# Combinations of h formed in place, one row behind each of the first two gates and queries, and convolution taps at 0.61 per us

## The chip, the cores and the metric

The kernel runs on one core of a Trainium2 chip. The metric is the device time of one execution in microseconds; the time of a kernel is the median of several executions. The engines named below are TensorE (PE; PEld is its weight load), VectorE (DVE), ScalarE (ACT), GpSimd (POOL) and SyncE (SP), whose only work here is to issue DMAs. DMAs are issued by SyncE, ScalarE and GpSimd and run on sixteen DMA engines.

## What is computed

One layer of a hybrid decoder on 1024 tokens and 16 meta tokens, model width 1024, in float32:

```python
h = rmsnorm(concat([meta, x]), norm_g)                # 1040 x 1024
glu_a, glu_b, z, q, f, i, g_rec, m_conv, m_rec = split(h @ w_in)   # nine sections of 1024
c = causal_dwconv31(glu_a * sigmoid(glu_b)) + conv_b
y_conv = (silu(layernorm(c)) * silu(z)) @ w_conv_out
f = lb + (1 - lb) * sigmoid(f);  k = 1 - f            # HGRN2, 8 heads of 128
o = recurrence(silu(q), k, decay f, values i)         # per head
y_rec = (group_rmsnorm(o) * silu(g_rec)) @ w_rec_out
x = x + (sigmoid(m_conv) * y_conv + sigmoid(m_rec) * y_rec) @ w_out
return rmsnorm(x, final_g)                            # the 1024 real tokens
```

## The kernel before

Channels lie on the partitions and tokens in the columns. h is kept as eight rows (k = 0 to 7), each 128 partitions x 1056 columns: two halves of 528 columns, the second of which repeats 16 tokens. Every matmul operand is split into a high and a low fp32r part, `hh[k]` and `hl[k]` for h; a product takes three matmuls (high x high, high x low, low x high). Weights come as 512 KB tiles: SyncE loads them into `wraw` (two buffers), ScalarE makes the high part and the negated copy of it, and GpSimd adds the raw tile to that by an accumulating DMA (`load_w`, `split_dma`, L139 to L141, L149).

Almost every larger tile is a slot of one pool, `big`: SLOTS = 35 slots of 128 x 1056 float32. A tile gets a slot when the slot's last user is done, and a DMA that still reads the old tile holds it. PSUM has two pools of four banks, `mm` for projections and `hg` for the recurrence. The compiling framework orders the instructions of every engine once, at compile time; each engine then runs its queue in that order. The order need not be the program's, so a row's place in a queue is read from the trace.

**First stage (up to about 480 us).** A list of jobs is run in order: for head j a gate f (`f_job`, wp[4, j]), a query q (`q_job`, wp[3, j]), for some j a quarter of v; then the first two GLU channels. A job's matmuls are cut into small pieces, and after each `tick()` advances the background work by the TensorE time that the piece takes: the recurrence of the previous heads (`hgrn`, a step each 2.0 us; its first step makes QD at L377, then score matmuls at L342), the convolution taps (`conv_taps`, L648) and sums of weights in DRAM (`weight_sums`, L718 and L720). A gate's four column blocks are evacuated by ScalarE (L575) and VectorE (L576, L578), a query's two by L596 and L597.

**Combinations of h.** The second stage multiplies 2 x 2 blocks of weights by 2 x 2 blocks of h with seven products instead of eight. Block row 1 of h is the rows k = 0 to 3, block row 2 the rows 4 to 7; the block columns are the two halves of 528. The products need four combinations, T4 to T7. `h_sums(k)` forms them for one k: it loads rows k and k + 4 of h from DRAM (`h_d`) into `ha` and `hb`, makes four differences and sums of 528 columns on VectorE (L738 to L741), splits each into high and low part (`tsum`, L135 and L136) and stores it to `t_d` in DRAM (L745). Its four calls are jobs: the first two after the first gate, the other two after the first query. At the end of the first stage `h_load` brings T4, T5 and T6 back into twelve slots `t` (L757), and T7 over the second halves of `hh` and `hl` (L762, L763).

**Second stage.** Sixteen gate units (`gate_unit`, one block of 512 columns) and six GLU units (`glu_unit`, two of 264), each of seven products (`strassen`, L879 to L883). Their pieces of weights are 256 KB. The taps of the eight channels are spread over the units by `tick()` at `CONV_RATE` taps per us of TensorE work (0.5 in the first stage); what is left is done at `drain(cbg)`, just before `ln_stats`. A channel's queue is 30 taps of 1024 columns (L648) and a last step that adds it to `csum`.

Of the kernel before, what the change touches and what calls it, by code (L numbers as in the profile page):

```python
# [8 lines left out]
F32 = mybir.dt.float32  # L9
F32R = mybir.dt.float32r  # L10
# [3 lines left out]
ALU = mybir.AluOpType  # L14
PSUM = bass.MemoryType.PSUM

P = 128
# [5 lines left out]
LH = 528  # L23
LX = 2 * LH
# [7 lines left out]
SLOTS = 35  # L32
NSPILL = 6
HG_GAP = 2.0
CONV_RATE = 0.64
SUM_GAP = 2.05
GLU_OVER = 14
EARLY_RATE = 0.5
# [6 lines left out]
def hybrid_kernel(ctx: ExitStack, tc: tile.TileContext, xT, xtok, wv, wp, wro, wco, wout, prm, fg, msk, out):  # L45
    nc = tc.nc
    act, dve, pe = nc.scalar, nc.vector, nc.tensor
# [6 lines left out]
    dram = ctx.enter_context(tc.tile_pool(name="dram", bufs=1, space=bass.MemoryType.DRAM))  # L54
# [8 lines left out]
    def slot(name, n=LX, dt=F32, parts=P):  # L63
        return big.tile([parts, n], dt, name=name, tag="s")
# [4 lines left out]
    def hg_bank():  # L69
# [23 lines left out]
                      in1=lbm.unsqueeze(1).broadcast_to([P, 2, KT]), op=ALU.subtract)  # L93
# [40 lines left out]
    def split(src, hi, lo):  # L134
        act.copy(out=hi, in_=src)  # L135
        dve.tensor_tensor(out=lo, in0=src, in1=hi.bitcast(F32), op=ALU.subtract)  # L136
# [194 lines left out]
    TT = dve.tensor_tensor  # L331
# [210 lines left out]
    hh, hl, hpair = [], [], []  # L542
    h_d = dram.tile([KT, P, LX], F32, name="h_d")
    jobs = []
# [20 lines left out]
    def f_job(j):  # L565
        def run(w):
            Fg = slot("F", L)
            K = slot("K", L)
            for blk in project(w, hh, hl, FB):
                yield  # L570
                if blk is None:
                    continue
                o, n, ps = blk
                fs = Fg[:, o:o + n]
                act.activation(out=fs, in_=ps[:, 0:n], func=AF.Sigmoid)  # L575
                dve.tensor_scalar(out=fs, in0=fs, scalar1=oml[:, j:j + 1], scalar2=lb[:, j:j + 1],  # L576
                                  op0=ALU.mult, op1=ALU.add)
                dve.tensor_scalar(out=K[:, o:o + n], in0=fs, scalar1=-1.0, scalar2=1.0,  # L578
                                  op0=ALU.mult, op1=ALU.add)
            head[j] = (Fg, K)  # L580
        return run

    def q_job(j):
        def run(w):
            while j > 0 and j - 1 not in placed:
                step(bg)
            QD = qx.tile([P, 3, 512], F32, name="QD", tag="qx")
            for blk in project(w, hh, hl, RB):
                yield
                if blk is None:  # L590
                    continue
                o, n, ps = blk
                h0 = o // 2
                qv = QD[:, 0:2, h0:h0 + n // 2].rearrange("p e j -> p j e")
                psv = ps.rearrange("p (j e) -> p j e", e=2)
                act.activation(out=qv, in_=psv, func=AF.Sigmoid)  # L596
                TT(out=qv, in0=psv, in1=qv, op=ALU.mult)  # L597
            bg.append(hgrn(j, *head.pop(j), QD))
        return run

    def v_job(q):
        def run(ws):
            if not hpair:
                hpair.extend(meta_pair(hh[k], hl[k], f"hpair{k}") for k in range(KT))
            yield from v_quarter(q, ws, hh, hl, hpair, False)
        return run
# [117 lines left out]

    t_d = {i: dram.tile([4, P, LX], F32, name=f"t{i}_d") for i in (4, 5, 6, 7)}
    tt = {4: [], 5: [], 6: []}

    def h_sums(k):  # L730
        def run(w):
            ha, hb = slot("ha"), slot("hb")
            nc.sync.dma_start(out=ha, in_=h_d[k])
            nc.sync.dma_start(out=hb, in_=h_d[k + 4])
            t7 = slot("t7", LH)
            b1, b2 = ha[:, 0:LH], ha[:, LH:LX]
            b3, b4 = hb[:, 0:LH], hb[:, LH:LX]
            TT(out=b1, in0=b1, in1=b2, op=ALU.subtract)  # L738
            TT(out=t7, in0=b4, in1=b2, op=ALU.subtract)
            TT(out=b4, in0=b1, in1=b4, op=ALU.add)  # L740
            TT(out=b3, in0=b4, in1=b3, op=ALU.subtract)  # L741
            for i, src in ((6, b4), (5, b1), (4, b3), (7, t7)):
                t = slot("tsum", dt=F32R).rearrange("p (a n) -> p a n", a=2)
                split(src, t[:, 0], t[:, 1])
                nc.gpsimd.dma_start(out=t_d[i][k], in_=t.rearrange("p a n -> p (a n)").bitcast(F32))  # L745
            yield
        return run

    def h_load():

        for i in (6, 5, 7, 4):
            for k in range(4):
                if i == 7:
                    h_last(k)
                    continue
                t = slot(f"t{i}_{k}", dt=F32R)
                nc.gpsimd.dma_start(out=t, in_=t_d[i][k])  # L757
                tt[i].append(t.rearrange("p (a n) -> p a n", a=2))
        yield

    def h_last(k):
        nc.gpsimd.dma_start(out=hh[k][:, LH:LX], in_=t_d[7][k][:, 0:LH])  # L762
        nc.gpsimd.dma_start(out=hl[k][:, LH:LX], in_=t_d[7][k][:, LH:LX])  # L763

    def drained():
        drain(bg)
# [2 lines left out]

    for j in range(NC):  # L770
        jobs.append(([wp[4, j]], f_job(j)))
        if j == 0:
            jobs.append(([], h_sums(0)))
            jobs.append(([], h_sums(1)))
        jobs.append(([wp[3, j]], q_job(j)))
        if j == 0:
            jobs.append(([], h_sums(2)))
            jobs.append(([], h_sums(3)))
        if j in (2, 4):
            q = j // 2 + 1  # L780
            jobs.append(([wv[q, 0], wv[q, 1]], v_job(q)))
    for j in range(2):
        jobs.append(([wp[1, j]], gb_job(j)))
        if j == 1:
            jobs.append(([], lambda w: drained()))
        jobs.append(([wp[0, j]], ga_job(j)))
    jobs.append(([], lambda w: h_load()))

    for i in range(2):
# [23 lines left out]
    first.close()  # L813
    rate[0] = CONV_RATE

# [509 lines left out]
```

## Time and profile before

| | |
|---|---|
| median of three runs | 1232.61 us (1230.66 to 1234.72) |
| the profiled execution, its own time | 1230.3 us |
| its span from the first to the last instruction | 1228.2 us |
| TensorE busy | 1163.5 us, 95% of the span |
| VectorE busy | 877.1 us, 71% |
| ScalarE busy | 588.0 us, 48% |
| GpSimd busy | 287.6 us, 23% |
| mean granted TensorE clock | 0.981 |

Busy time is a share of one execution. Matmuls are pipelined and their ends are modelled, so a busy TensorE can still be a slow one; the granted clock says at what share of full speed it ran.

### The profile page before, as it was taken

What the parts mean: (1) busy time and instruction counts of PE and PEld (TensorE: products, weight loads), DVE (VectorE), ACT (ScalarE), POOL (GpSimd) and SP (SyncE); (2) the same over time, 40 slices, a digit from 0 to 9 for tenths busy, and PEclk for the clock granted to TensorE, in tenths of its full rate; (3) what the DMA queues carried; (4) which work ended last, traced back from release to release, by engine and by line L of the source; (5) the groups of instructions that cost most, each with busy time, mean ns of one, the idle gap of its engine ahead of it and who ended that gap; (6) DMA issues with size and microseconds to landing.
All of it is one profiled execution on the core that took longest, in us unless ns stands there. A gap on an engine that the chain in (4) does not pass through costs nothing.

```text
span 1228.2 us, 21742 instructions
## 1 busy us (share of the span) xinstructions
PE 1163.5 (95%) x8376; PEld 1008.0 (82%) x8376; DVE 877.1 (71%) x1501; ACT 588.0 (48%) x1063; POOL 287.6 (23%) x376
## 2 busy tenths in 40 slices
PE   8994999989999999699999999999999899999997
PEld 7984789979988898478898978988888678888886
DVE  7457766367366589796999997698989747645444
ACT  7563342433533422377767668585855534323211
POOL 5242021322222233212222222322233231000000
PEclk9996999999999999899999999999999999999999
DMA  6479587999699996988998999988899896545321
GB/s 219 155 229 369 174 217 196 228 225 263 161 222 212 200 199 175 358 222 232 253 241 239 224 232 260 215 217 208 228 232 349 285 272 230 181 121 182 118 86 52
DMA packets 119223, 266.54 MB, mean 217 GB/s; under 512 B 12112, under 2 KB 12496, under 8 KB 119120
## 3 DMA queue, kind: packets, MB, share of 16 engines
q0 software_dynamic: 49264, 123.16, 45.1%
q1 hardware_dynamic: 60496, 125.07, 30.4%
q10 hardware_dynamic: 9360, 16.94, 3.8%
q8 instruction: 65, 1.06, 0.3%
q14 instruction: 38, 0.31, 0.1%
HBM read 169.04 MB, written 95.81 MB: 216 GB/s over the span
## 4 chain that ended last, share of the span: by engine, by line
PE 73%; DVE 11%; DMA 10%; issue 3%; ACT 1%; POOL 1%; SPq 0%; DVEq 0%; POOLq 0%; ACTq 0%
PE mm L320 8%; PE mm L323 8%; PE mm L324 8%; PE hg L879 5%; PE hg L882 5%; PE hg L883 5%; PE mm L883 5%; PE mm L879 5%; PE mm L882 4%; DVE c L648 2%; PE mm L204 2%; PE mm L206 2%; PE mm L205 2%; DMA hb<-h_d 2%; DMA wr<-sum_rec 1%
## 5 line engine op out<-in xcount | busy, mean ns | idle before, releaser
L648 DVE SCALAR_TENSOR_TENSOR c<-glu,pt,c 128x1024 f32<-128x1024 f32 (+10 forms) x240 | 306.3, 1279 | 3.6
L141 POOL DMA_DIRECT2D wl<-wr x129 | 110.9, 897 | 329.2 <-ACT wl L140 255.2
L320 PE MATMUL mm<-hh,whi 128*128 128x264 f32 (+2 forms) x512 | 166.2, 326 | 12.0 <-ACT F L575 11.6
L323 PE MATMUL mm<-hl,whi 128*128 128x264 f32 (+2 forms) x512 | 162.4, 318 | 0.5 <-DVE hl L559 0.5
L324 PE MATMUL mm<-hh,wlo 128*128 128x264 f32 (+2 forms) x512 | 161.1, 315 | 0.0
L139 ACT CAST wh<-wr 128x512 fp32r<-128x512 f32 x129 | 78.1, 618 | 108.4 <-PE hg L882 44.5
L320 PEld LDWEIGHTS mm<-hh,whi 128*128 128x128 f32 x512 | 98.4, 193 | 19.0 <-ACT F L575 11.8
L323 PEld LDWEIGHTS mm<-hl,whi 128*128 128x128 f32 x512 | 98.4, 192 | 6.4 <-DVE hl L559 1.2
L324 PEld LDWEIGHTS mm<-hh,wlo 128*128 128x128 f32 x512 | 98.4, 192 | 5.6
L883 PE MATMUL mm<-hh,wl 128*128 128x512 f32 (+1 forms) x224 | 78.1, 349 | 4.7 <-DMA wl<-wr 4.7
L879 PE MATMUL hg<-hh,wh 128*128 128x512 f32 (+1 forms) x224 | 78.8, 352 | 3.6 <-DVE e L909 3.0
L879 PE MATMUL mm<-hh,wh 128*128 128x512 f32 (+1 forms) x224 | 78.4, 350 | 2.3 <-ACT wh L139 1.9
L140 ACT ACTIVATE wl<-wh 128x512 fp32r<-128x512 f32 x129 | 79.6, 629 | 1.7
L883 PE MATMUL hg<-hh,wl 128*128 128x512 f32 (+1 forms) x224 | 78.4, 350 | 0.4 <-DVE wl L136 0.4
L882 PE MATMUL hg<-hl,wh 128*128 128x512 f32 (+1 forms) x224 | 78.5, 350 | 0.0
L882 PE MATMUL mm<-hl,wh 128*128 128x512 f32 (+1 forms) x224 | 78.0, 348 | 0.0
L135 ACT CAST wh<-wr 128x512 fp32r<-128x512 f32 x63 | 38.7, 619 | 51.5 <-PE mm L323 29.2
L879 PE MATMUL hg<-t,wh 128*128 128x512 f32 (+1 forms) x168 | 58.9, 351 | 1.7 <-DMA t<-t_d 1.7
L883 PE MATMUL mm<-t,wl 128*128 128x512 f32 (+1 forms) x168 | 58.9, 351 | 1.0 <-DMA wl<-wr 1.0
L879 PE MATMUL mm<-t,wh 128*128 128x512 f32 (+1 forms) x168 | 59.0, 351 | 0.8 <-ACT wh L135 0.8
L882 PE MATMUL mm<-t,wh 128*128 128x512 f32 (+1 forms) x168 | 58.9, 350 | 0.0
L882 PE MATMUL hg<-t,wh 128*128 128x512 f32 (+1 forms) x168 | 58.7, 349 | 0.0
(346 smaller groups left out, 3095.7 us busy)
## 6 DMA issues: line engine op xcount, KB each, us to landing
wl<-wr POOLq DMA_DIRECT2D x129, 256.0 KB, 5.0
wr<-in_wp_dram SPq DMA_DIRECT2D x66, 256.0 KB, 3.9
wlo<-wraw POOLq DMA_DIRECT2D x24, 512.0 KB, 7.3
wraw<-in_wp_dram SPq DMA_DIRECT2D x20, 512.0 KB, 5.8
t_d<-tsum POOLq DMA_DIRECT2D x16, 528.0 KB, 7.9
sum_rec<-in_wp_dram SPq DMA_DIRECT2D x16, 512.0 KB, 10.5
sum_z<-in_wp_dram SPq DMA_DIRECT2D x16, 512.0 KB, 8.0
wr<-sum_rec SPq DMA_DIRECT2D x32, 256.0 KB, 4.2
```

What stands on the lines that cost most here:

```text
L135: act.copy(out=hi, in_=src)
L139: act.copy(out=hi, in_=src)
L140: act.activation(out=lo, in_=hi.bitcast(F32), func=AF.Copy, scale=-1.0)
L141: nc.gpsimd.dma_start(out=lo, in_=src, accum_op=ALU.add)
L204: pe.matmul(ps, lhsT=a, rhs=whi, start=first, stop=False, **kw)
L320: mm = pe.matmul(ps[:, 0:n], lhsT=a, rhs=xh[k][:, o:o + n], start=(k == 0), stop=False)
L323: pe.matmul(ps[:, 0:n], lhsT=a, rhs=xl[k][:, o:o + n], start=False, stop=False)
L324: last[:] = [pe.matmul(ps[:, 0:n], lhsT=b, rhs=xh[k][:, o:o + n], start=False, stop=(k == KT - 1))]
L648: dve.scalar_tensor_tensor(out=dst, in0=a[:, p0 - d:L - d], scalar=cw[:, j, TAPS - 1 - d:TAPS - d], in1=dst, op0=ALU.mult, op1=ALU.add)
L879: mm = pe.matmul(ps[c], lhsT=a, rhs=xh, start=start and k == 0, stop=False, skip_group_check=True)
L882: pe.matmul(ps[c], lhsT=a, rhs=xl, start=False, stop=False, skip_group_check=True)
L883: pe.matmul(ps[c], lhsT=b, rhs=xh, start=False, stop=k == 3, skip_group_check=True)
```

## The change

`h_sums` no longer takes a seventh slot for T7: all four combinations replace the blocks of `ha` and `hb` that they come from, so `ha` ends as T5 and T7 and `hb` as T4 and T6. Each of the two tiles is then split in one piece of 1056 columns: ScalarE casts it into a slot `tsum`, which is stored as the high part, and VectorE subtracts that from the tile in place, which is stored as the low part. A row takes four slots. `t_d` becomes one tensor in which the two combinations of a tile lie side by side, so a load of T4, T5 or T6 reads two pieces of 528 columns a partition.

The four rows are placed differently among the jobs: one behind the first gate, one behind the first query, one behind the second gate, one behind the second query. `CONV_RATE` goes from 0.64 to 0.61.

```diff
--- before.py
+++ after.py
@@ -32,7 +32,7 @@
 SLOTS = 35
 NSPILL = 6
 HG_GAP = 2.0
-CONV_RATE = 0.64
+CONV_RATE = 0.61
 SUM_GAP = 2.05
 GLU_OVER = 14
 EARLY_RATE = 0.5
@@ -724,7 +724,9 @@
 
 
 
-    t_d = {i: dram.tile([4, P, LX], F32, name=f"t{i}_d") for i in (4, 5, 6, 7)}
+
+    t_d = dram.tile([4, P, 4, 2, LH], F32, name="t_d")
+    place = {5: (0, 0), 7: (0, 1), 4: (2, 0), 6: (2, 1)}
     tt = {4: [], 5: [], 6: []}
 
     def h_sums(k):
@@ -732,35 +734,34 @@
             ha, hb = slot("ha"), slot("hb")
             nc.sync.dma_start(out=ha, in_=h_d[k])
             nc.sync.dma_start(out=hb, in_=h_d[k + 4])
-            t7 = slot("t7", LH)
             b1, b2 = ha[:, 0:LH], ha[:, LH:LX]
             b3, b4 = hb[:, 0:LH], hb[:, LH:LX]
             TT(out=b1, in0=b1, in1=b2, op=ALU.subtract)
-            TT(out=t7, in0=b4, in1=b2, op=ALU.subtract)
+            TT(out=b2, in0=b4, in1=b2, op=ALU.subtract)
             TT(out=b4, in0=b1, in1=b4, op=ALU.add)
             TT(out=b3, in0=b4, in1=b3, op=ALU.subtract)
-            for i, src in ((6, b4), (5, b1), (4, b3), (7, t7)):
-                t = slot("tsum", dt=F32R).rearrange("p (a n) -> p a n", a=2)
-                split(src, t[:, 0], t[:, 1])
-                nc.gpsimd.dma_start(out=t_d[i][k], in_=t.rearrange("p a n -> p (a n)").bitcast(F32))
+            for i, src in ((2, hb), (0, ha)):
+                t = slot("tsum", dt=F32R)
+                act.copy(out=t, in_=src)
+                nc.gpsimd.dma_start(out=t_d[k][:, i].rearrange("p a n -> p (a n)"), in_=t.bitcast(F32))
+                TT(out=src, in0=src, in1=t.bitcast(F32), op=ALU.subtract)
+                nc.gpsimd.dma_start(out=t_d[k][:, i + 1].rearrange("p a n -> p (a n)"), in_=src)
             yield
         return run
 
     def h_load():
 
         for i in (6, 5, 7, 4):
+            r, c = place[i]
             for k in range(4):
                 if i == 7:
-                    h_last(k)
+                    for part, dst in enumerate((hh[k], hl[k])):
+                        nc.gpsimd.dma_start(out=dst[:, LH:LX], in_=t_d[k][:, r + part, c])
                     continue
-                t = slot(f"t{i}_{k}", dt=F32R)
-                nc.gpsimd.dma_start(out=t, in_=t_d[i][k])
-                tt[i].append(t.rearrange("p (a n) -> p a n", a=2))
+                t = slot(f"t{i}_{k}", dt=F32R).rearrange("p (a n) -> p a n", a=2)
+                nc.gpsimd.dma_start(out=t, in_=t_d[k][:, r:r + 2, c])
+                tt[i].append(t)
         yield
-
-    def h_last(k):
-        nc.gpsimd.dma_start(out=hh[k][:, LH:LX], in_=t_d[7][k][:, 0:LH])
-        nc.gpsimd.dma_start(out=hl[k][:, LH:LX], in_=t_d[7][k][:, LH:LX])
 
     def drained():
         drain(bg)
@@ -769,13 +770,11 @@
 
     for j in range(NC):
         jobs.append(([wp[4, j]], f_job(j)))
-        if j == 0:
-            jobs.append(([], h_sums(0)))
-            jobs.append(([], h_sums(1)))
+        if j < 2:
+            jobs.append(([], h_sums(2 * j)))
         jobs.append(([wp[3, j]], q_job(j)))
-        if j == 0:
-            jobs.append(([], h_sums(2)))
-            jobs.append(([], h_sums(3)))
+        if j < 2:
+            jobs.append(([], h_sums(2 * j + 1)))
         if j in (2, 4):
             q = j // 2 + 1
             jobs.append(([wv[q, 0], wv[q, 1]], v_job(q)))
```

## Rows read from the trace of the kernel before

**Rows 1.** The page: the chain that ended last, shares of the span by engine.
```profile
PE 73%; DVE 11%; DMA 10%; issue 3%; ACT 1%; POOL 1%; SPq 0%; DVEq 0%; POOLq 0%; ACTq 0%
```

**Rows 2.** Busy time by stage; columns in the first line, DMA share and GB/s last.
```profile
core 0: us, PE busy (x) PEld busy (x) DVE busy (x) ACT busy (x) POOL busy (x), PEclk, DMA share, GB/s
75.00:100.00 25.00, 18.46 (x157) 15.99 (x156) 12.47 (x20) 10.31 (x15) 3.93 (x6) 0.87 0.88 282
100.00:125.00 25.00, 12.72 (x133) 11.60 (x132) 18.98 (x38) 8.18 (x15) 8.23 (x14) 0.70 1.01 366
...
480.00:500.00 20.00, 12.92 (x52) 8.68 (x52) 14.45 (x21) 8.91 (x15) 6.39 (x12) 0.90 0.85 291
500.00:540.00 40.00, 33.92 (x132) 26.59 (x132) 36.34 (x38) 20.91 (x32) 8.98 (x11) 0.92 0.90 280
580.00:640.00 60.00, 60.00 (x341) 52.38 (x341) 57.05 (x70) 42.48 (x67) 15.57 (x19) 1.00 0.95 241
```

**Rows 3.** Waits of TensorE in 74 to 130 us: total, times, longest.
```profile
PE mm L320 <- ACT F L575: 11.6, 1, 11.6
PE hg L342 <- DVE QD L377: 6.5, 1, 6.5
```

**Rows 4.** Busy time right after the two waits, columns as in rows 2.
```profile
98.00:104.00 6.00, 6.00 (x80) 5.88 (x69) 6.00 (x12) 2.33 (x4) 2.15 (x4) 0.53 1.05 337
...
121.00:128.00 7.00, 6.28 (x76) 4.69 (x77) 7.00 (x20) 0.76 (x3) 1.30 (x3) 0.54 0.98 338
```

**Rows 5.** The chain within 74 to 130 us: shares by line, one piece (start, duration).
```profile
by line: DMA hb<-h_d 40.6%; DMA wlo<-wraw 13.7%; DVE tsum L136 6.6%; issue 5.0%; DVE hb L740 5.0%; DVE t L739 4.9%; ACT tsum L135 4.0%; PE hg L342 4.0%; DVE QX L386 3.1%; DVE hb L741 3.0%; PE mm L323 2.9%; PE mm L324 2.3%; PE mm L320 2.0%; 
...
107.88 8.96 DMA hb<-h_d
```

**Rows 6.** VectorE in order of time, 95 to 98 us: start, duration, instruction, wait.
```profile
96.19 0.71 DVE L739 TENSOR_TENSOR t<-hb,ha 128x528 f32<-128x528 f32 x1 [1.23 <-DMA hb<-h_d]
96.82 0.69 DVE L377 TENSOR_TENSOR QD<-QD,F 128x512 f32<-128x512 f32 x1
```

**Rows 7.** ScalarE in order of time, 118 to 122 us, columns as in rows 6.
```profile
118.41 0.63 ACT L135 CAST tsum<-hb 128x528 fp32r<-128x528 f32 x1 [6.94 <-DVE hb L740]
...
120.55 1.21 ACT L575 ACTIVATE F<-mm 128x264 f32<-128x264 f32 x4
```

**Rows 8.** Waits of SyncE's queue in 74 to 160 us, columns as in rows 3.
```profile
SPq L149 <- DMA wlo<-wraw: 95.9, 7, 23.9
SPq L734 <- DMA t_d<-tsum: 7.0, 2, 6.1
```

**Rows 9.** Issues of SyncE in order of time, 40 to 140 us, columns as in rows 6.
```profile
86.83 0.33 SPq L149 DMA_DIRECT2D wraw<-in_wp_dram  x1
...
122.44 0.33 SPq L149 DMA_DIRECT2D wraw<-in_wv_dram  x1
```

**Rows 10.** Groups by line and shape, whole span: total busy us, mean ns, idle before.
```profile
L648 DVE SCALAR_TENSOR_TENSOR c<-glu,pt,c 128x1024 f32<-128x1024 f32 x128 | 164.3, 1284 | 2.2
L141 POOL DMA_DIRECT2D wl<-wr x129 | 110.9, 897 | 329.2 <-ACT wl L140 255.2 <-PE mm L883 20.0 <-DMA gmc_d<-e 7.4
...
L720 POOL DMA_DIRECT2D sum_rec<-in_wp_dram x8 | 10.7, 1527 | 0.2 <-issue 0.2
...
L559 DVE TENSOR_TENSOR hl<-h,hh 128x1056 fp32r<-128x1056 f32 x8 | 10.0, 1253 | 2.6 <-ACT hh L557 1.6 <-DMA h_d<-h 0.9
```

**Rows 11.** GpSimd's DMA queue: packets, MB, share; 474 to 477, then 488 to 496.
```profile
q0 software_dynamic: 415, 0.79, 100.4%
...
q0 software_dynamic: 529, 1.97, 70.0%
```

**Rows 12.** Waits of TensorE in 480 to 580 us, columns as in rows 3.
```profile
PE mm L883 <- DMA wl<-wr: 5.7, 4, 3.1
...
PE hg L879 <- DMA t<-t_d: 1.7, 1, 1.7
```

**Rows 13.** VectorE in order of time, 946 to 962 us, columns as in rows 6.
```profile
960.58 0.69 DVE L1077 TENSOR_TENSOR cr<-cr,hg 128x512 f32<-128x512 f32 x1 [6.10 <-DMA cr<-c_d]
```

## The prediction

> **What bounds the kernel now.** I read the page's chain first: TensorE makes 73% of it, so a change is worth what it returns to TensorE or takes from it [rows 1]. The table by stage then shows where TensorE is not busy: 6.5 us are missing in 75 to 100 us, 12.3 in 100 to 125, 7.1 in 480 to 500 and 6.1 in 500 to 540. From 580 to 640 nothing is missing, though VectorE is busy 57 of 60 us [rows 2]. The combinations of h are formed in the first of these places and read back in the 480s, so I queried both.
>
> In 74 to 130 us TensorE waits in two long pieces, 6.5 and 11.6 us [rows 3]. After each the granted clock is about half, 1.2 instead of 2.4 GHz: 0.53 in 98 to 104 and 0.54 in 121 to 128. Work that holds TensorE for 6.00 us at 0.53 costs 6.00 x 0.47 = 2.8 us extra, 6.28 us at 0.54 costs 2.9 [rows 4]. So the first gap costs 6.5 + 2.8 = 9.3 us, the second 11.6 + 2.9 = 14.5, together 23.8.
>
> Who ends the gaps? The chain of this stretch is mostly the load of hb, 40.6% of it, 9.0 us of it in one piece [rows 5]. In VectorE's queue L377, the first recurrence head's opening, stands behind L739 of row 1, which waits for hb; the score matmuls L342 wait for L377, and that is the first gap [rows 3, 6]. In ScalarE's queue the four evacuations of the second gate (L575) stand behind the four casts of row 3, which wait 6.9 us for VectorE's work on hb. The gate's four blocks fill all four PSUM banks of `mm` until then, and the next query's matmuls wait: the second gap [rows 3, 7].
>
> Why is hb late? SyncE's own waits give two reasons: 95.9 us in seven waits of weight loads, for buffers that the accumulating DMA of the low parts still reads, and 7.0 us of hb's load for a slot that a store of `tsum` still holds [rows 8]. So row 1's loads go out behind a weight load that left at 86.83 [rows 9], and the last hb at 107.88 only [rows 5].
>
> The slots explain the second reason. At the first row 23 of 35 are taken for long: 16 of hh and hl, four v tiles, vm, F and K. Twelve are left, and a row wants seven (ha, hb, t7, four of tsum). Two rows don't fit, and F and K of the second gate, which come after all four rows in the program, queue for what is left.
>
> **What the change takes away and adds.**
> *Row arithmetic.* Before, a row is eight operations of 528 columns on VectorE, four TT and four subtractions, of about 0.71 us each [rows 6], and four casts of 0.63 on ScalarE [rows 7]. After, it is the same four TT, then two subtractions of 1056 columns, which by the nearest row take 1.25 us [rows 10]: 5.7 becomes 5.3 us, 1.4 us over four rows. ScalarE casts the same columns in half as many instructions. Both lie off the path outside the gaps and I count them as nothing; stores and loads of h_d keep their bytes.
>
> *Four slots a row, and rows 2 and 3 behind the second gate and query.* Three rows now fit in the twelve slots, and F and K of the second gate come after two rows instead of four. The second gap loses both its parents: row 3 is no longer ahead of L575, and hb no longer waits for stores. The gain lies between 0 (another row takes row 3's place, a rival) and 14.5; I take 14.5, because fewer slots and a later place both act on it.
>
> The first gap belongs to row 1, which stays close to where it was. If its loads keep their place in SyncE's queue, behind the weight load of 86.83 [rows 9], the gap stays; if they move ahead of it, because rows 0 and 1 together now want eight slots where they wanted fourteen, it goes. Between 0 and 9.3 I take half, 4.7: no row tells which.
>
> *What is queued behind the rows now.* Rows 2 and 3 fall among the steps of the first recurrence head. VectorE was already busy 19.0 of 25 us there [rows 2], and a row's 5.3 us ahead of a step delays score matmuls that TensorE takes in order. At best VectorE catches up and it costs 0; at worst one row's 5.3 us shows. I take 2.5.
>
> *The loads of T4, T5 and T6.* A partition's share of a load is now two pieces of 2112 bytes in DRAM instead of one of 4224. Where only 2112-byte pieces ran (the loads into hh and hl), 0.79 MB took 100.4% of sixteen engines for 3 us: 3.8 us a MB. Where nearly only 4224-byte pieces ran on that queue, 1.97 MB took 70.0% of 8 us: 2.8 us a MB [rows 11]. Twelve loads are 6.5 MB, so up to 6.3 us more, where TensorE waits 1.7 us for t and 5.7 for wl behind it [rows 12]. On GpSimd an issue may grow too: between an accumulating DMA of 128 pieces, 0.90 us, and one of 256, 1.53 us, lie 0.63 us, 7.6 for twelve [rows 10]. Some of both hides under the first product, which needs no t; the bounds are 0 and 13.9. The packets are the nearer row, and about half of their 6.3 us may be hidden: I take 3.
> The Trainium skill, page "DMA: Bandwidth & Descriptors", section "Why small descriptors are slow (HBM only)", gives each packet a fixed 3 cycles or so beside its 32 bytes a cycle: splitting costs, but hardly here. By that a 4224-byte row is 135 cycles and two halves are 138, as an estimate 2% or 0.4 us over twelve loads, and the sum would come out 2.6 us lower. The trace disagrees: its two rates differ by a third.
>
> *Taps at 0.61.* A step of convolution taps is about 1.28 us of VectorE [rows 10]. Counting by the kernel's own units (17.92 for a gate, 18.48 for a GLU unit, 238 steps left when the rate changes), 7 steps are left for the drain at 0.64 and 8 at 0.61: at 0.64, 25 steps find no tap ready, at 0.61 14. One more tap falls there, 1.28 us, under the 6.1 us that VectorE then waits for reloaded convolution rows [rows 13]; without that cover it would cost its 1.28. In return VectorE has some 2 us less to do in 60, and may evacuate a little sooner after 500 us. Bounds -2 to +1.3, taken as 0.
>
> **Sum.** 1230.3 of the profiled execution (span 1228.2 and 2.1 around it) - 14.5 - 4.7 + 2.5 + 3 = 1216.6. The median of the runs shown lies 2.3 above that execution: 1219. What is won at 120 us stays won, as TensorE is the bound up to 480 and its work paces what runs beside it.
>
> **The rivals.**
> *Both gaps go.* For it: the rows want fewer slots everywhere. Against: row 1 stands behind a wait for a weight buffer, which no slot shortens. 1230.3 - 23.8 + 3 + 2.3 = 1212.
> *A later row takes row 3's place.* The casts of row 2 or 3 land in ScalarE's queue ahead of an evacuation again, with hb 9 us away, and the 14.5 is paid once more: 1219 + 14.5 = 1233, no change. For: all the queues are in order, and where a row lands in them is the compiler's choice. Against: fewer slots are held. Then the change would not do what it says.
> *The loads cost their upper bound.* 13.9 instead of 3: 1230, no change. Against: TensorE waited for t itself only 1.7 us.
> *Slower: a row's load behind a long weight wait.* SyncE stands from 108.2, when hb is out [rows 5], to 122.4 at one weight load [rows 9], 14.2 us, and up to 23.9 us at another [rows 8]. If hb of row 2 or 3 comes behind such a wait while its arithmetic already stands in VectorE's queue, head 0's steps stop TensorE for as long and the slow clock follows. From a stop of about 14 us on the forecast's gain is gone; 14.2 + 2.9 gives 1236, 23.9 + 2.9 gives 1246.
>
> **How the numbers follow.** Forecast 0.47, both gaps 0.27, a later row 0.12, costly loads 0.05, slower 0.09. The forecast's own bounds (first gap 0 to 9.3, backlog 0 to 5.3, loads 0 to 7, not all at once) make 1211 to 1228. The range of eight in ten reaches from 1206 (both gaps gone, loads free, taps at -2) to 1232 (most of a later row's price). A change of 0.3% is 3.7 us, about what can be told from no change. Faster, under 1228.9, takes the first two and a third of the later row: 0.78. The rest of that row and the costly loads are the same, 0.13; slower 0.09.
>
> **What would show it.** No wait of TensorE for L575 and a granted clock of 1.0 in 110 to 128; no wait of SyncE for a store of `t_d`; sixteen stores of 528 KB still, and no t7. The first gap shows as a wait of L342 for L377. If the loads cost, t's landing and TensorE's missing time in 480 to 540 grow beyond today's 13.2 us. The forecast is wrong if casts of `tsum` stand right before a late evacuation again, or if TensorE waits anew between 110 and 200.

## The result, and the profile after

The kernel after takes 1219.3 us (median of four runs, 1217.8 to 1222.0), the one before 1232.6 on the same chip. The ratio is 0.9894, with a 95% interval of 0.9868 to 0.9920: 1.1% faster. The profiled execution takes 1217.8 us, its span is 1216.0.

The waits of TensorE in 74 to 130 us of the kernel after, columns as in [rows 3]:

```profile
PE hg L342 <- DVE QD L377: 8.2, 1, 8.2
PE hg L484 <- DVE K L469: 0.5, 1, 0.5
```

The wait for L575 is gone, all 11.6 us of it. The wait of L342 for L377, the first gap, is not smaller but 1.7 us longer than in [rows 3]. Busy time by stage, of the kernel after, columns as in [rows 2]:

```profile
75.00:100.00 25.00, 16.78 (x135) 14.42 (x138) 10.99 (x15) 8.24 (x9) 4.87 (x7) 0.88 0.85 271
100.00:125.00 25.00, 24.53 (x323) 21.16 (x312) 24.07 (x59) 9.25 (x16) 3.74 (x7) 0.92 0.84 265
480.00:500.00 20.00, 14.85 (x59) 10.06 (x57) 14.27 (x14) 8.20 (x13) 5.70 (x9) 1.00 1.16 385
500.00:540.00 40.00, 35.49 (x141) 27.92 (x140) 38.49 (x41) 25.38 (x36) 9.03 (x11) 0.91 0.93 262
```

In 100 to 125 TensorE now misses 0.5 of 25 us where it missed 12.3, in 75 to 100 it misses 8.2 instead of 6.5, and from 480 to 540, where the second stage is ten us further on, 9.7 instead of 13.2 [rows 2]. The granted clock behind the two places, of the kernel after, the same columns:

```profile
94.00:104.00 10.00, 4.92 (x80) 4.80 (x81) 7.98 (x12) 2.34 (x3) 0.55 (x1) 0.50 0.89 305
121.00:128.00 7.00, 6.53 (x36) 5.26 (x35) 5.86 (x8) 3.29 (x6) 0.83 (x2) 1.00 0.84 258
```

121 to 128 runs at 2.4 GHz now, where it was 0.54 of that [rows 4]. The first gap still costs its slow clock: 8.2 + 4.92 x 0.50 = 10.7 us, against the 9.3 of before.

Why the second gap went can be read in ScalarE's order, columns as in [rows 7], kernel after:

```profile
100.84 1.08 ACT L745 CAST tsum<-hb 128x1056 fp32r<-128x1056 f32 x1 [9.19 <-DVE hb L742]
101.83 1.08 ACT L745 CAST tsum<-ha 128x1056 fp32r<-128x1056 f32 x1
102.80 0.38 ACT L575 ACTIVATE F<-mm 128x264 f32<-128x264 f32 x1
104.88 0.39 ACT L575 ACTIVATE F<-mm 128x264 f32<-128x264 f32 x1 [1.70 <-PE mm L324]
```

The second gate's evacuations now stand behind the casts of row 1, whose hb has landed, and from the second on they wait for TensorE itself. Row 1's casts still wait 9.19 us, but none of TensorE's waits is for what they hold up. Why the first gap stayed stands in SyncE's order and then in VectorE's, kernel after:

```profile
87.11 0.33 SPq L149 DMA_DIRECT2D wraw<-in_wp_dram  x1
87.55 0.72 SPq L735 DMA_DIRECT2D ha<-h_d  x1
88.36 0.38 SPq L736 DMA_DIRECT2D hb<-h_d  x1
```

```profile
95.14 0.71 DVE L739 TENSOR_TENSOR ha<-ha 128x528 f32<-128x528 f32 x1 [4.81 <-DMA ha<-h_d]
95.77 1.07 DVE L597 TENSOR_TENSOR QD<-mm,QD 128x512 f32<-128x512 f32 x1
97.72 0.71 DVE L740 TENSOR_TENSOR ha<-hb,ha 128x528 f32<-128x528 f32 x1 [0.87 <-DMA hb<-h_d]
98.34 0.68 DVE L377 TENSOR_TENSOR QD<-QD,F 128x512 f32<-128x512 f32 x1
```

Row 1's loads leave behind the same weight load, at 87.11 where it was 86.83 [rows 9], and L377 still stands behind L739 and L740, which wait for them. The longer wait, 4.81 us, is for ha. So it was in the kernel before, whose VectorE waited 3.47 us for ha at L738 and then 1.23 for hb at L739 [rows 6]:

```profile
93.27 0.71 DVE L738 TENSOR_TENSOR ha<-ha 128x528 f32<-128x528 f32 x1 [3.47 <-DMA ha<-h_d]
```

The start of the first score matmuls (L342) of four heads, and of the second stage's first matmul, read from TensorE's order of time in each trace, in us; the runs are those of the experiments below:

| | head 0 | head 1 | head 2 | head 4 | second stage | end |
|---|---|---|---|---|---|---|
| before | 97.6 | 157.2 | 199.3 | 295.7 | 484.6 | 1228.2 |
| rate_only | 98.8 | 154.7 | 199.6 | 296.1 | 484.8 | 1228.4 |
| after | 99.1 | 144.6 | 185.3 | 285.7 | 474.1 | 1216.0 |
| after_rate064 | 101.1 | 146.6 | 187.2 | 285.7 | 473.8 | 1218.5 |
| place_only | 97.6 | 145.8 | 184.1 | 283.1 | 471.6 | 1217.0 |
| inplace_only | 99.2 | 155.2 | 197.9 | 295.6 | 483.3 | 1228.5 |
| row1_loads_with_row0 | 96.2 | 143.6 | 186.1 | 283.9 | 471.8 | 1214.5 |
| row1_later | 93.4 | 143.9 | 187.0 | 285.7 | 473.6 | 1218.8 |
| act_loads | 92.5 | 143.5 | 187.0 | 284.8 | 472.7 | 1215.2 |
| whole_loads | 98.8 | 144.3 | 187.6 | 285.6 | 474.1 | 1218.8 |
| no_arithmetic | 90.9 | 135.6 | 178.6 | 275.8 | 464.5 | 1211.8 |

Each row is one execution. rate_only differs from before, and after_rate064 from after, in the second stage alone, so what their starts differ by in the first stage, up to 2.5 us, is the difference from one execution to the next.

From before to after the stretches between these points change by +1.5, -14.1, -1.4, +4.0, -0.5 and -1.7 us: together -12.2, the whole difference of the spans. Of the 14.0 won at head 2, four are given back by head 4. There TensorE misses 4.8 us in 100.4 instead of 3.8 in 96.4, and its mean granted clock is 0.97 instead of 1.00, from two short stretches, of the kernel after:

```profile
193.00:197.00 4.00, 4.00 (x79) 3.71 (x78) 0.96 (x7) 0.38 (x2) 0.20 (x1) 0.58 0.27 104
251.00:254.00 3.00, 3.00 (x47) 2.88 (x36) 3.00 (x13) 0.00 (x0) 0.21 (x1) 0.50 0.88 224
```

100.4 x 0.03 + 1.0 = 4.0. The first of the two follows a pause of TensorE of 1.8 us that the waits put down to nothing. The same stretch took 98.5 us in after_rate064, 99.0 in place_only and 97.8 in act_loads, so part of it belongs to one execution; what of it is the change's stays open.

### The profile page after: what moved, and what is told of

It reads as the page before. It is cut to its first block, busy times and chain, and to the rows that moved or that the text cites. A ratio compares the mean times of both kernels' runs of the same rounds, so it can differ in the third digit from the quotient of the medians.

```text
span 1216.0 us, 21734 instructions
## 1 busy us (share of the span) xinstructions
PE 1162.0 (96%) x8376; PEld 1005.9 (83%) x8376; DVE 876.8 (72%) x1493; ACT 587.0 (48%) x1055; POOL 289.9 (24%) x376
## 4 chain that ended last, share of the span: by engine, by line
PE 65%; DMA 9%; DVE 8%; issue 4%; ACT 1%; POOL 1%; DVEq 0%; ACTq 0%; POOLq 0%; SPq 0%
PE mm L320 7%; PE mm L323 7%; PE mm L324 7%; PE mm L882 5%; PE mm L878 5%; PE mm L881 5%; PE hg L878 4%; PE hg L881 4%; PE hg L882 4%; DMA wl<-wr 2%; PE mm L204 1%; DMA rl<-rl_d 1%; DMA t<-t_d 1%; DMA cr<-c_d 1%; PE mm L205 1%
```

## The experiments

Each ran in five rounds beside the kernel before. Ratios are to before, with the 95% interval. A diff is against the kernel after where nothing else is said.

**Which part pays?** Three kernels make one part of the change each, or all but one. place_only is the kernel before, against which its diff stands, with the new order of jobs alone:

```diff
-        if j == 0:
-            jobs.append(([], h_sums(0)))
-            jobs.append(([], h_sums(1)))
+        if j < 2:
+            jobs.append(([], h_sums(2 * j)))
         jobs.append(([wp[3, j]], q_job(j)))
-        if j == 0:
-            jobs.append(([], h_sums(2)))
-            jobs.append(([], h_sums(3)))
+        if j < 2:
+            jobs.append(([], h_sums(2 * j + 1)))
```

> The kernel before with only the new order of jobs: one row behind each of the first two gates and queries, still seven slots a row, the old t_d, taps at 0.64. If the place of row 3 alone made the second gap (its casts ahead of the second gate's evacuation), the 11.6 us wait for L575 is gone and the time is about 1219 (1216 to 1223). If the slots made it, loads of hb still wait some 7 us for stores of tsum, a wait of that size comes back at another place, and the time is 1226 to 1233.

1219.2 against 1231.9 us: 0.9896 (0.9878 to 0.9914), all of the gain. Its waits in SyncE's queue, 74 to 160 us, columns as in [rows 8]:

```profile
SPq L149 <- DMA wlo<-wraw: 66.2, 6, 17.0
SPq L733 <- DVE tsum L136: 6.9, 2, 6.2
```

Loads still wait 6.9 us for slots, as long as the 7.0 of [rows 8], and it costs nothing that shows: TensorE's only long wait here is the first gap, 6.8 us.

inplace_only is the other half: the new combinations, t_d and its loads, in the old order of jobs and with the taps at 0.64.

```diff
-CONV_RATE = 0.61
+CONV_RATE = 0.64
...
-        if j < 2:
-            jobs.append(([], h_sums(2 * j)))
+        if j == 0:
+            jobs.append(([], h_sums(0)))
+            jobs.append(([], h_sums(1)))
         jobs.append(([wp[3, j]], q_job(j)))
-        if j < 2:
-            jobs.append(([], h_sums(2 * j + 1)))
+        if j == 0:
+            jobs.append(([], h_sums(2)))
+            jobs.append(([], h_sums(3)))
```

> The new kernel's combinations (four slots a row, t_d in one tensor) in the old order of jobs, two rows behind the first gate and two behind the first query, taps at 0.64. If the slots made the second gap, it goes: SyncE no longer waits for stores and the time is about 1219. If the place made it, row 3's casts still stand ahead of L575; only the 7 to 8 us for which hb waited for slots may go, so a wait of 4 to 9 us is left and the time is 1224 to 1231.

1231.0 against 1231.9: 0.9988 (0.9974 to 1.0003), nothing that can be told. Waits of TensorE in 74 to 130 us, then ScalarE and SyncE in order of time, all of inplace_only:

```profile
PE mm L320 <- ACT F L575: 9.8, 1, 9.8
PE hg L342 <- DVE QD L377: 8.7, 1, 8.7
```

```profile
118.21 1.07 ACT L745 CAST tsum<-hb 128x1056 fp32r<-128x1056 f32 x1 [3.59 <-DVE hb L742]
119.19 1.07 ACT L745 CAST tsum<-ha 128x1056 fp32r<-128x1056 f32 x1
120.16 1.21 ACT L575 ACTIVATE F<-mm 128x264 f32<-128x264 f32 x4
```

```profile
105.41 0.33 SPq L149 DMA_DIRECT2D wraw<-in_wv_dram  x1
105.92 0.90 SPq L735 DMA_DIRECT2D ha<-h_d  x1
106.98 1.20 SPq L736 DMA_DIRECT2D hb<-h_d  x1
```

No load waits for a store here, yet row 3's hb leaves at 106.98, 0.9 us before the 107.88 of [rows 5], because the load in front of it in SyncE's queue waits for its weight buffer. Row 3's casts stand ahead of the four L575 as in [rows 7], and the gap stays. The wait for slots lay inside the wait for the weight buffer. SyncE's order in the kernel before says the same:

```profile
96.42 0.32 SPq L734 DMA_DIRECT2D hb<-h_d  x1
105.09 0.33 SPq L149 DMA_DIRECT2D wraw<-in_wv_dram  x1
```

The long wait for a slot (6.1 of the 7.0 us) is that of row 2's hb, which left at 96.42. The weight load behind it, ahead of row 3's loads, stood at its own buffer until 105.09.

rate_only and after_rate064 change one line, in the kernel before and in the kernel after:

```diff
-CONV_RATE = 0.64
+CONV_RATE = 0.61
```

```diff
-CONV_RATE = 0.61
+CONV_RATE = 0.64
```

> The kernel before with only the taps at 0.61 in the place of 0.64. By the prediction one more tap falls to the drain, under a wait: 1232.6 within 1.5 us. By the rival, that fewer taps ahead of the second stage's evacuations give TensorE time back, 1227 to 1230.

> The changed kernel with the taps back at 0.64. By the prediction 1219 within 1.5 us, as changed. By the rival the 1.7 us that the second half of the trace came out shorter than the first half explains are the taps', and the time is 1221 to 1223.

rate_only: 1231.3 against 1231.9, 0.9997 (0.9982 to 1.0012). after_rate064: 1220.3, 0.9905 (0.9885 to 0.9925), whose interval holds after's 0.9894. The taps' rate does nothing that can be measured.

**What keeps the first gap?** Three kernels bring row 1's data earlier, or its arithmetic later. row1_loads_with_row0 issues row 1's two loads with row 0's, ahead of the weight load of 87.11:

```diff
-            ha, hb = slot("ha"), slot("hb")
-            nc.sync.dma_start(out=ha, in_=h_d[k])
-            nc.sync.dma_start(out=hb, in_=h_d[k + 4])
+            for r in ((0, 1) if k == 0 else () if k == 1 else (k,)):
+                ab = slot("ha"), slot("hb")
+                nc.sync.dma_start(out=ab[0], in_=h_d[r])
+                nc.sync.dma_start(out=ab[1], in_=h_d[r + 4])
+                loaded[r] = ab
+            ha, hb = loaded.pop(k)
```

> The changed kernel, but the loads of ha and hb of row 1 are issued together with those of row 0, so ahead of the weight load at 87 us; everything else stays, and L377 still stands behind row 1's arithmetic in VectorE's queue. If the first gap (8.2 us in the changed kernel) is the lateness of row 1's load, it falls below 3 us and its slow clock goes: 1219 - 8 - 2.9 = 1208 to 1212. If it is VectorE's own work, or DMA that is full whoever comes first, the gap stays above 6 us: 1217 to 1221.

1216.7 against 1232.6: 0.9878 (0.9855 to 0.9901). The first gap falls to 5.1 us, between the two forecasts. The interval overlaps after's, so no gain over it is shown. VectorE in order of time, of row1_loads_with_row0 (row 1's first operation is L744 here):

```profile
89.27 0.70 DVE L744 TENSOR_TENSOR ha<-ha 128x528 f32<-128x528 f32 x1
...
95.43 0.69 DVE L377 TENSOR_TENSOR QD<-QD,F 128x512 f32<-128x512 f32 x1
```

Row 1 waits for no load any more. But from L744 to L377 VectorE works without a pause: two subtractions of row 0, three operations of row 1 and L597 stand between them. So the late load makes some 3 of the 8.2 us, and in what is left VectorE's own work on the rows stands ahead of the head.

row1_later puts the rows behind the first gate, the second gate, the second query and the third gate:

```diff
-        if j < 2:
-            jobs.append(([], h_sums(2 * j)))
+        if j < 3:
+            jobs.append(([], h_sums((0, 1, 3)[j])))
         jobs.append(([wp[3, j]], q_job(j)))
-        if j < 2:
-            jobs.append(([], h_sums(2 * j + 1)))
+        if j == 1:
+            jobs.append(([], h_sums(2)))
```

> The changed kernel with row 1 behind the second gate, row 2 behind the second query and row 3 behind the third gate, so that no row but row 0 stands ahead of L377 of head 0. If a waiting row ahead of L377 makes the first gap, it goes: 1208 to 1212. The rival is that the wait moves with the row: row 2 now stands ahead of L377 of head 1, and a wait of L342 of 4 to 9 us comes there: 1215 to 1221.

1220.1: 0.9892 (0.9874 to 0.9911). Waits of TensorE in 92 to 145 us, then VectorE in order of time, of row1_later:

```profile
PE hg L537 <- DVE on L527: 6.3, 1, 6.3
PE hg L342 <- DVE QD L377: 3.0, 1, 3.0
```

```profile
127.80 0.71 DVE L739 TENSOR_TENSOR ha<-ha 128x528 f32<-128x528 f32 x1 [6.58 <-DMA ha<-h_d]
```

Head 0's scores start 5.7 us earlier than after's. But row 2's L739 now waits 6.58 us for ha in VectorE's queue, with the head's closing steps (L523 to L527) behind it, and TensorE stands 6.3 us for those before it can transpose the head's output (L537). At head 1 only 0.7 us of the lead is left.

act_loads gives the rows' loads to ScalarE's queue, past the weight loads:

```diff
-            nc.sync.dma_start(out=ha, in_=h_d[k])
-            nc.sync.dma_start(out=hb, in_=h_d[k + 4])
+            nc.scalar.dma_start(out=ha, in_=h_d[k])
+            nc.scalar.dma_start(out=hb, in_=h_d[k + 4])
```

> The changed kernel with ha and hb loaded from ScalarE's queue instead of SyncE's, so that no weight load's wait stands ahead of them. If waits for weight buffers in SyncE's queue make the rows late, the first gap falls below 3 us: 1207 to 1212. If the rows are late for other reasons (full DMA, ScalarE's own order), the time stays at 1217 to 1222, and waits of ScalarE come instead.

1218.9: 0.9882 (0.9861 to 0.9904). TensorE's waits in 92 to 145 us, and VectorE in order of time, of act_loads:

```profile
PE hg L516 <- DVE S L504: 3.7, 1, 3.7
PE hg L342 <- DVE QD L377: 2.7, 1, 2.7
```

```profile
126.83 0.36 DVE L504 SCALAR_TENSOR_TENSOR S<-S,PA,hg 128x128 f32<-128x128 f32 x1
131.15 0.71 DVE L739 TENSOR_TENSOR ha<-ha 128x528 f32<-128x528 f32 x1 [3.97 <-DMA ha<-h_d]
131.78 0.34 DVE L504 SCALAR_TENSOR_TENSOR S<-S,PA,hg 128x128 f32<-128x128 f32 x1
```

The same thing at another step: an L739 stands in the middle of the state updates L504 and waits 3.97 us, so L516, the head's output matmuls, waits 3.7. The kernel is 6.6 us ahead of after at head 0 and 1.1 at head 1. VectorE is busy 42.9 of the 51 us between the two; it is the wait in its queue that gives the lead back, not its work.

**What do the split loads cost?** whole_loads gives t_d an order in DRAM in which a partition's share of a load of T4 to T6 is one piece of 4224 bytes again, and the stores write two of 2112:

```diff
-    t_d = dram.tile([4, P, 4, 2, LH], F32, name="t_d")
-    place = {5: (0, 0), 7: (0, 1), 4: (2, 0), 6: (2, 1)}
+    t_d = dram.tile([4, P, 2, 2, 2, LH], F32, name="t_d")
+    place = {5: (0, 0), 7: (0, 1), 4: (1, 0), 6: (1, 1)}
...
-                t = slot(f"t{i}_{k}", dt=F32R).rearrange("p (a n) -> p a n", a=2)
-                nc.gpsimd.dma_start(out=t, in_=t_d[k][:, r:r + 2, c])
+                t = slot(f"t{i}_{k}", dt=F32R)
+                nc.gpsimd.dma_start(out=t, in_=t_d[k][:, r, c].rearrange("p a n -> p (a n)"))
```

> The changed kernel with another layout of t_d: the stores write pieces of 2112 bytes and the loads of T4 to T6 read one piece of 4224 again. If the split loads cost what the prediction took (3 us), the time falls to 1215 to 1217 and the landing of t by some 2 us; if they are hidden, it stays within 1.5 us of 1219.3.

1219.6: 0.9886 (0.9868 to 0.9905), the same as after. The loads, by the trace's groups of DMA issues (the last number is the median time in us from issue to landing, when the data have arrived), first the kernel after, then whole_loads:

```profile
t<-t_d POOLq DMA_DIRECT2D x12, 528.0 KB, 14.3
```

```profile
t<-t_d POOLq DMA_DIRECT2D x12, 528.0 KB, 14.2
```

**Does more distance help?** one_a_head puts the rows behind the first gate and the second, third and fourth query; late_heads behind the second to fifth query.

```diff
-        if j < 2:
-            jobs.append(([], h_sums(2 * j)))
+        if j in {0: 0}:
+            jobs.append(([], h_sums({0: 0}[j])))
         jobs.append(([wp[3, j]], q_job(j)))
-        if j < 2:
-            jobs.append(([], h_sums(2 * j + 1)))
+        if j in {1: 1, 2: 2, 3: 3}:
+            jobs.append(([], h_sums({1: 1, 2: 2, 3: 3}[j])))
```

For late_heads the first table is empty and the second is {1: 0, 2: 1, 3: 2, 4: 3}.

> The changed kernel with the rows spread further: row 0 behind the first gate, rows 1 to 3 behind the second, third and fourth query, so head 0 starts with one row instead of three beside it. If a waiting row ahead of a recurrence step is all that costs, and fewer rows per head let VectorE keep up, the first gap falls to the 3 us that the evacuation of the query itself takes and nothing takes its place: 1207 to 1212. If whatever is given back there is lost again by the next row, behind L377 or L527 of a later head, 1215 to 1221.

> The changed kernel with the rows behind the queries 1 to 4, none beside the start of head 0. First gap at most 3 us and no row in 90 to 115 us. By the theory that a row costs what it makes VectorE wait ahead of a recurrence step, each of the four can still cost 2 to 5 us: 1207 to 1214. By the rival, that the stretch from 90 to 145 us is bound by something else than the rows, the second score group still starts at 143 to 145 us and the time is 1216 to 1221.

Both are slower than before, which no forecast of theirs had allowed for: one_a_head takes 1238.6 against 1233.5, 1.0045 (1.0023 to 1.0067), and late_heads 1244.5, 1.0101 (1.0072 to 1.0131). TensorE's waits in 74 to 360 us and VectorE in order of time, of one_a_head; then the waits of late_heads:

```profile
PE hg L342 <- DVE QD L377: 13.1, 2, 9.9
PE hg L516 <- ACT S L502: 8.2, 1, 8.2
PE hg L537 <- DVE on L527: 6.5, 3, 4.7
```

```profile
243.28 0.71 DVE L739 TENSOR_TENSOR ha<-ha 128x528 f32<-128x528 f32 x1 [12.04 <-DMA oT_d<-oT]
```

```profile
PE hg L537 <- DVE on L527: 15.9, 3, 10.8
PE hg L342 <- DVE QD L377: 9.1, 2, 8.9
PE hg L516 <- ACT S L502: 8.0, 1, 8.0
```

These waits sum to 27.8 and 33.0 us; those of the same lines in after are 8.4, 0.4 and none. The L739 of rows 1 to 3 wait 3.6, 4.9 and 12.0 us in one_a_head, those of rows 0 to 3 2.8 to 11.2 in late_heads, each ahead of a head's step. In the 8.2 us of L516 the row's casts wait in ScalarE's queue ahead of L502, which the head needs. The profile puts the 12.04 down to another transfer, but the wait ends as ha lands: ha left at 230.50, behind three weight sums in SyncE's order, and landed 12.7 us later, where the median of ha in after is 6.6. The order, then the issue with its time to landing, of one_a_head:

```profile
228.51 1.88 SPq L718 DMA_DIRECT2D sum_glu<-in_wp_dram  x3
230.50 0.54 SPq L735 DMA_DIRECT2D ha<-h_d  x1
```

```profile
ha<-h_d SPq DMA_DIRECT2D x1, 528.0 KB, 12.7
```

**What could the rows still give?** no_arithmetic keeps the places of the rows, their loads and their stores, and leaves out the combinations, the subtractions and the casts with their slots:

```diff
-            TT(out=b1, in0=b1, in1=b2, op=ALU.subtract)
...
-                t = slot("tsum", dt=F32R)
-                act.copy(out=t, in_=src)
-                nc.gpsimd.dma_start(out=t_d[k][:, i].rearrange("p a n -> p (a n)"), in_=t.bitcast(F32))
-                TT(out=src, in0=src, in1=t.bitcast(F32), op=ALU.subtract)
+                nc.gpsimd.dma_start(out=t_d[k][:, i].rearrange("p a n -> p (a n)"), in_=src)
```

> The changed kernel with the rows' arithmetic left out: ha and hb are loaded and each is stored twice as it is, without the four combinations, casts and subtractions, so the second stage computes with other numbers; all DMAs stay. If VectorE's wait for hb and its 5.3 us a row are what is left to win, the first gap falls to 3 us and the time to 1206 to 1212. If full DMA or the order of weight loads bounds the stretch, the time stays at 1215 to 1220.

1214.3 against 1233.5: 0.9850 (0.9818 to 0.9882), between its two forecasts. That is some 5 us under after, though the two intervals still overlap. The first gap is 0.9 us, and the second stage starts 9.6 us earlier than after's, of which the end keeps 4.2. Busy time in 465 to 580 us, columns as in [rows 2], first the kernel after, then no_arithmetic, then whole_loads:

```profile
465.00:580.00 115.00, 99.72 (x509) 81.65 (x508) 95.58 (x121) 65.05 (x101) 32.33 (x42) 0.97 0.95 272
```

```profile
465.00:580.00 115.00, 102.28 (x479) 83.08 (x479) 91.84 (x108) 67.81 (x106) 31.20 (x39) 0.93 0.91 261
```

```profile
465.00:580.00 115.00, 100.11 (x499) 82.06 (x497) 93.73 (x118) 63.90 (x100) 29.28 (x41) 0.93 0.91 265
```

In no_arithmetic TensorE is busy longer at a lower granted clock: 115 x 0.04 = 4.6 us, near the 5.4 that are given back. That the earlier start makes the clock lower is not shown: whole_loads begins its second stage at 474.1, as after does, and its clock is 0.93 too. What the loss comes from stays open.

## Why the prediction was right, and where it was not

The forecast of 1219 stands, and the main step with it: the second gap went, with its slow clock. 14.1 us are won between the scores of heads 0 and 1, where 14.5 were counted. So close a match is partly luck: in rate_only, with the first stage of before, the second gap is 8.4 us instead of 11.6, and from its 55.9 us between these heads to after's 45.5 only 10.4 are won. Under the total three terms were off. They were counted as -4.7 + 2.5 + 3 = +0.8 and came out near +1.4, and that they cancel is luck too.

- **Second gap, -14.5: right, for one of the two reasons given.** "Fewer slots and a later place both act on it" is half wrong. place_only shows that the place alone gives it all, though a load there still waits 6.9 us for a slot; inplace_only shows that the slots alone give nothing. "The slots explain the second reason" was read from 7.0 us of SyncE's waits [rows 8], without asking whether the queue would have been free without them: it would have stood at a weight buffer until 105.4.
- **First gap, -4.7: mis-sized.** It measured +1.4 (9.3 became 10.7), and the wait is 6.5 and 7.8 us in before and rate_only, 8.2 and 9.1 in after and after_rate064: it did not shrink. The rival's argument held: row 1 stands behind a weight load, which no slot shortens. Half of a gap for which no row spoke was a mean, not a mechanism. The reading was too narrow as well: it named L739's wait for hb, 1.23 us, and left out L738's for ha, 3.47 us, which stands before it. Nor does the gap go when the loads move ahead of the weight load, as the prediction had it: 5.1 us stay in row1_loads_with_row0. The experiments add that the term could hardly have been had: shortened to 5.1, 3.0 and 2.7 us, the gap gave no gain over after that its measurement tells. In row1_later and act_loads another row's L739 waited ahead of a later step; in row1_loads_with_row0 no later row waits, and why its lead of 2.9 us at head 0 is about 1 at head 1 stays open.
- **VectorE's backlog, +2.5: about 0.** VectorE is busy 24.1 of 25 us in 100 to 125, but TensorE misses 0.5 there. Between heads 0 and 1 after takes 45.5 us, and no_arithmetic, without the rows' arithmetic at all, 44.7.
- **Split loads, +3: about 0.** whole_loads is the same within its interval, and the loads land after 14.3 and 14.2 us. GpSimd's issue did grow, from a median of 0.56 to 0.74 us, nearer its lower bound. TensorE's waits in 465 to 580 us for t and wl grew from 1.7 and 5.7 to 3.1 and 7.4, but from the second stage's first matmul to the end the executions with whole loads (before, rate_only, place_only, whole_loads) take 743.6 to 745.4 us, and those with split loads, no_arithmetic aside, 741.9 to 745.2: nothing of the 3 shows there. Two rates of a queue taken from two stretches [rows 11] had been read as a price of the piece. The Trainium skill, page "DMA: Bandwidth & Descriptors", section "Why small descriptors are slow (HBM only)", states a fixed overhead of about 3 cycles for each packet. The estimate that the prediction worked out from it, 2% or 0.4 us over the twelve loads, agrees with the landings, and the sentence that the trace disagreed does not hold.
- **Row arithmetic and taps, 0: right**, the taps by rate_only and after_rate064; the casts and subtractions were not tried apart from the rest of inplace_only, which gives nothing.
- **What is won stays won: not quite.** 14.0 us at head 2, 10.0 at head 4, 12.2 at the end.
- **The slower rival was a real mechanism, at another place.** In after the L739 of rows 2 and 3, at 119.24 and 134.34, start without a wait. row1_later, act_loads, one_a_head and late_heads show it step by step, up to 12 us a row. Its cause was named too narrowly, as a weight buffer. A load's own time to landing is enough: 12.7 us in one_a_head, and in act_loads, from ScalarE's queue, row 3's ha left at 122.11 and L739 ran at 131.15.

## What to carry to other kernels

Where queues run in order, first ask which instruction waits for a DMA ahead of an evacuation or a recurrence step, and move that instruction; freeing buffers helps only if the load would then really leave earlier, which the queue that issues it must show. Here a helper had a best place, not a best distance: too early it blocked one engine, too late it waited ahead of the next head's steps on another. And a gap that is removed counts only as far as the next meeting point of the engines: compare starts of the same matmul in both traces, head by head, before putting a gap's whole length into a sum. Two executions of the same first stage differed by up to 2.5 us at such a point, so a single trace does not settle a term of that size.

## What the runs showed of the hardware that was not expected

Twelve loads of 528 KB whose pieces in DRAM were halved from 4224 to 2112 bytes landed after 14.3 us (median) instead of 14.2, and the issue on GpSimd took 0.74 instead of 0.56 us. The mean granted clock of TensorE in 465 to 580 us was 0.97 in after and 0.93 in whole_loads, though both begin the second stage at 474.1 us. From there to the end they took 741.9 and 744.7 us.
